# The first gate/up pair by seven products, the frames' sums made earlier, the last forms spread

## The chip, the cores and the metric

The kernel runs on one core of one Trainium2 chip, in one launch. The metric is device time in microseconds (us), the median of several executions. All times below are us unless marked otherwise.

## The reference

One layer of a hybrid streaming encoder, for 512 prompt frames and 64 frames of a running stream (576 in all), D = 2048 channels, everything in float32:

```python
hn   = rmsnorm(x, g_norm1);  proj = hn @ w_in          # 2048 x 6144: q, k, v and three convolution inputs
o    = concat(rmsnorm(attention(q, k, v)), rmsnorm(gated short convolution))
x    = x + o @ w_out                                    # 2048 x 2048
h2   = rmsnorm(x, g_norm2)
x    = x + (silu(h2 @ w_gate) * (h2 @ w_up)) @ w_down   # D_FF = 5632
```

The change touches what lies between `x + o @ w_out` and the start of `@ w_down`.

## The kernel before, in words

**Precision.** A float32 matmul is made as three matmuls in the fast fp32r form: each operand is split into a high part and a rest, and high x high, rest x high, high x rest are summed in PSUM. `split` makes both parts: ACT casts the high part (L231), DVE subtracts it from the source (L232). Every weight block and every frame block passes through it.

**Seven products.** The 576 frames are taken in two halves of 288, and a unit of work is 256 columns of weights. Weights, frames and results are cut in 2 x 2 blocks, and the four blocks of the result are made from seven products (Strassen's scheme in Winograd's form) instead of eight. A product has 8 k-tiles of three matmuls, 24 matmuls of 128x128 by 128x288 (L406). It uses a sum of weight blocks and a sum of frame blocks. The weight sums are made for every unit on DVE (`weight_sums`, L344 to L354, four sums of 128x1024). The frame sums are made once for all gate and up units: t1 and t2 (tile `t12`, products 5 and 6) and t3 and t4 (`t34`, products 7 and 4).

**Order.** TensorE's order is written by hand: a list `order` of pairs (unit, product). `prepare(n, p)` issues loads, sums and splits of the weights of a product, and runs four entries ahead (`AHEAD`) of `run(n, p)`, which issues the matmuls and what follows them: a product's bank is copied out by ACT (`part`, L429), added by DVE to the other product of its result block, and given to `finish`. `Pipeline` spreads other work between the matmuls: it counts a tick for every three matmuls, and a generator that is spawned there goes on after as many ticks as it yields. The order on ACT, DVE, GpSimd and SP's DMA queue is set by a scheduler from its own costs, apart from the end (from product 1 of unit NGU-1, the last up unit, on), where all of them keep program order (`manual_schedule`). Every engine works its list in order.

**Feed-forward stage.** Gate and up units alternate, so pair `fp` has a gate and an up unit. `finish` scales a result block by the row scale R2 of the second RMSNorm, applies Silu for gate, and multiplies up by gate. `put_forms` then builds the seven sums ("forms") of the hidden block that the down projection will need, splits each into a 128x2x288 tile and stores it to DRAM (`hid_dram`, 288 KB each); they come back in loads of 2016 KB as the down units need them (SBUF doesn't hold them all). For the last pair, the forms with index over 3 are split into tiles that later are accumulators of the down stage (`spare`: `acc_ax`, `acc_t`, `acc_z`).

**Around the change.** `out_proj` (for the second half of channels, `mixa`) runs over eight blocks of 256 output channels, two channel tiles each, for both halves of frames, 96 matmuls a block; a result leaves through one of three PSUM banks by two DVE steps (L1022, L1023: scale and residual). `after_b2(kt)` then makes the high and low parts of the scaled x (h2: also the block b12), its square, and a running sum of squares on GpSimd (L1259), and stores x to DRAM for the later residual. Behind `out_proj` pair 0 of gate/up is made by eight full products in `wide` (L1391, 384 matmuls, four weight blocks of their own), with R2 made by `row_scale2` in between and the generator `frame_sums` making t12 and t34, one pair of channel tiles every nine ticks. Only then comes the loop over `order`, whose first two units are written interleaved:

```python
order = [(0, 1), (0, 2), (1, 1), (1, 2), (0, 6), (0, 7), (0, 5), (0, 3), (0, 4), (1, 6), (1, 7), (1, 5)]
```

Units of `w_in`, earlier in the kernel (numbers below zero, stage A), run through the same helpers; their first two units are interleaved too (`early=True`: product 3 has a bank `psv` of its own).

Of the kernel before, what the change touches and what calls it, by code (L numbers as in the profile page):

```python
# [10 lines left out]
F32 = mybir.dt.float32  # L11
# [90 lines left out]
def tile_hybrid_stream_step(  # L102
# [47 lines left out]
    for w in (w_gate, w_up):  # L150
        for kk in range(2):
            specs.append((w[kk * 1024 : (kk + 1) * 1024, 0:256].rearrange("(k p) c -> p k c", p=P), 8, 256))
# [190 lines left out]
    def weight_sums(n):  # L343

        st, m, tt = unit[n], UNITS[n][3], nc.vector.tensor_tensor
        st["a21"], st["a22"] = (region[n, 1][0][:, :, q, :] for q in range(2))
        st["s1"] = spool[0].tile([P, NP, P], F32, tag="s1", name="s1")[:, :m]
        tt(out=st["s1"], in0=st["a21"], in1=st["a22"], op=ALU.add)
        yield
        tt(out=st["a21"], in0=st["a21"], in1=st["a11"], op=ALU.subtract)  # L350
        yield
        tt(out=st["a11"], in0=st["s1"], in1=st["a11"], op=ALU.subtract)
        yield 6
        tt(out=st["a12"], in0=st["a12"], in1=st["a11"], op=ALU.subtract)  # L354
        yield 3
# [67 lines left out]
    def run(n, p_, early=False):  # L423
# [589 lines left out]
    def out_proj(frame, R, after=None):  # L1013
        for c in range(D // 256):
            whi, wlo = next_weight()
            load_x2()
            for j in range(2):
# [219 lines left out]
    b12pool = tc.alloc_tile_pool(name="b12pool", bufs=1, reuse_waits="tile", side="left")  # L1237
    b12h = b12pool.tile([P, NP, HALF], F32R, name="b12h")
    b12l = b12pool.tile([P, NP, HALF], F32R, name="b12l")
    acc2 = [b12pool.tile([P, HALF], F32, name=f"acc2_{i}") for i in range(2)]  # L1240

    def h2(kt, i):
        if i == 0:
            return h2a[kt]
        return b22s[kt // 2] if kt % 2 else (b12h[:, kt // 2, :], b12l[:, kt // 2, :])

    def after_b2(kt):
        for i, (a, b) in enumerate(HALVES):
            hi, lo = h2(kt, i)
            src = x2(kt)[:, a:b]  # L1250
            nc.scalar.activation(out=hi, in_=src, func=AF.Copy, scale=col("g2", kt))
            nc.vector.scalar_tensor_tensor(out=lo, in0=src, scalar=col("g2", kt), in1=hi.bitcast(F32),
                                           op0=ALU.mult, op1=ALU.subtract)
# [13 lines left out]
    parts2 = []  # L1267
    for i in range(2):
        sh, sl = parts("sq2")
        split(sh, sl, acc2[i])  # L1270
        parts2.append((sh, sl))
# [12 lines left out]
    t12z = tpool.tile([P, 2, 2, HALF], F32R, tag="t12z", name="t12z")  # L1284
    t34 = []
# [5 lines left out]
    turn = [0]  # L1291

    def ps_tile(name):
        turn[0] += 1
        if turn[0] % 2:
            return ps_pj.tile([P, HALF], F32, tag="pj", name=name)
        return ps_z.tile([P, 512], F32, tag=f"z{turn[0] // 2 % 3}", name=name)[:, :HALF]

    def frame_sums():

        for j in range(NP):
            ev, od = x2(2 * j), x2(2 * j + 1)
            ge, go = col("g2", 2 * j), col("g2", 2 * j + 1)
            b11 = tmp.tile([P, HALF], F32, tag="ms", name="b11", bufs=1)
            b22 = tmp.tile([P, HALF], F32, tag="t", name="b22", bufs=1)
            nc.scalar.activation(out=b11, in_=ev[:, :HALF], func=AF.Copy, scale=ge)
            nc.scalar.activation(out=b22, in_=od[:, HALF:], func=AF.Copy, scale=go)
            ta = b12pool.tile([P, 2, HALF], F32, tag="ta", name="ta")
            tb = b12pool.tile([P, 2, HALF], F32, tag="tb", name="tb")
            t1, t2, t3, t4 = ta[:, 0], ta[:, 1], tb[:, 0], tb[:, 1]  # L1310
            nc.vector.scalar_tensor_tensor(out=t1, in0=ev[:, HALF:], scalar=ge, in1=b11, op0=ALU.mult, op1=ALU.subtract)
            nc.gpsimd.tensor_tensor(out=t2, in0=b22, in1=t1, op=ALU.subtract)
            nc.vector.scalar_tensor_tensor(out=t3, in0=ev[:, HALF:], scalar=ge, in1=b22, op0=ALU.mult, op1=ALU.subtract)
            nc.vector.scalar_tensor_tensor(out=t4, in0=od[:, :HALF], scalar=go, in1=t2, op0=ALU.mult, op1=ALU.subtract)
            two = t12[:, :, j] if j < NP - 1 else t12z
            split(two[:, :, 0, :], two[:, :, 1, :], ta)
            t34.append(ypool.tile([P, 2, 2, HALF], F32R, tag=f"y{j}", name=f"t34_{j}"))
            split(t34[j][:, :, 0, :], t34[j][:, :, 1, :], tb)
            yield 9

# [3 lines left out]
    spare = []  # L1324

    def put_form(fp, n, src):

        if fp == NFP - 1 and n > 3:
            t = spare.pop(0)()
        else:  # L1330
            t = tmp.tile([P, 2, HALF], F32R, tag="hl", name="form")
# [28 lines left out]

    def finish(kind, fp, c, i, ps, part=None):
# [8 lines left out]
        else:  # L1370
            nc.vector.tensor_tensor(out=s, in0=ps, in1=part, op=ALU.add)  # L1371
            nc.vector.tensor_tensor(out=s, in0=s, in1=R2[:, a:b], op=ALU.mult)
        if kind == "gate":
            nc.scalar.activation(out=s, in_=s, func=AF.Silu)
            return
# [4 lines left out]
    def wide(kind, hold=None):  # L1380

        pss = {}
        for kk in range(2):
            whi, wlo = next_weight()
            for i, j in ((1, 0), (1, 1), (0, 0), (0, 1)):
                if kk == 0:
                    pss[j, i] = ps_tile("pw")
                for k in range(8):
                    xh, xl = h2(8 * kk + k, i)
                    for n, (w_, x_) in enumerate(((whi, xh), (wlo, xh), (whi, xl))):  # L1390
                        mm(pss[j, i], w_[:, k, j * P : (j + 1) * P], x_,  # L1391
                           start=(kk == 0 and k == 0 and n == 0), stop=(kk == 1 and k == 7 and n == 2))
                    pipe.tick()
                if kk == 1:
                    finish(kind, 0, j, i, pss[j, i])
            if hold and kk == 0:
                hold()
# [45 lines left out]
    down = {}  # L1443

    def take_blocks(d):

        if d in (0, 3):
# [17 lines left out]
    def spare_tile(name, q):  # L1465

        if name not in down:
            pool, n, tag = {"z": (h2pool, 6, "z"), "t": (tpool, 4, "t12z"), "ax": (down["pool"], 2, "ax")}[name]
            down[name] = pool.tile([P, n, HALF], F32, tag=tag, name=f"acc_{name}")
        return down[name][:, 2 * q : 2 * q + 2, :].bitcast(F32R)  # L1470

    for name, q in (("ax", 0), ("t", 0), ("t", 1), ("z", 2)):
        spare.append(lambda name=name, q=q: spare_tile(name, q))
# [64 lines left out]
    for k_ in range(AHEAD):  # L1538
        prepare(*order[k_])
    for k_, (n, p_) in enumerate(order):  # L1540
# [5 lines left out]
        run(n, p_)  # L1546
# [62 lines left out]
```

## Time and profile before

| | |
|---|---|
| median of 3 runs | 2394.09 (2393.43 to 2395.15) |
| profiled execution, its own time | 2397.15 |
| span of its trace | 2395.4 |
| granted TensorE clock, mean | 0.995 |
| instructions in the span | 43789 |
| TensorE matmuls | 17609, busy 2350.2 |

Stages by the trace: units of w_in from about 80 to 600, attention and the first half of `out_proj` to 784, the second half to 886.70, `wide` to 938.18, seven-product units of gate/up to about 1880, down units to about 2388.

How to read the rows. In a row of time order stand start, duration, engine, line, operation, output<-input, tile size, count, and in brackets the idle time ahead of it and what ended it. In a group (line first) stand the count, busy time and mean ns of one, then the idle time ahead and what ended it. In a row of windows stand the stretch, its length, busy time and count of TensorE, of its weight loads, of DVE, ACT and GpSimd, the granted clock, the busy share of the DMA engines and GB/s. In a wait stand who waits, for whom, total, times, longest. In a DMA row stand issues, KB each, and median us from issue to landing. Matmul durations overlap (each row shows about 0.29 while one starts every 0.132), so the length of a group is its count times 0.132. A 288-wide step is 128 partitions by 288 elements.

### The profile page before, as it was taken

What the parts mean: (1) busy time and instruction counts of PE and PEld (TensorE: products, weight loads), DVE (VectorE), ACT (ScalarE), POOL (GpSimd) and SP (SyncE); (2) the same over time, 40 slices, a digit from 0 to 9 for tenths busy, and PEclk for the clock granted to TensorE, in tenths of its full rate; (3) what the DMA queues carried; (4) which work ended last, traced back from release to release, by engine and by line L of the source; (5) the groups of instructions that cost most, each with busy time, mean ns of one, the idle gap of its engine ahead of it and who ended that gap; (6) DMA issues with size and microseconds to landing.
All of it is one profiled execution on the core that took longest, in us unless ns stands there. A gap on an engine that the chain in (4) does not pass through costs nothing.

```text
span 2395.4 us, 43789 instructions
## 1 busy us (share of the span) xinstructions
PE 2350.2 (98%) x17609; PEld 2336.2 (98%) x17609; DVE 1934.0 (81%) x2828; ACT 1234.6 (52%) x2211; POOL 300.3 (13%) x377
## 2 busy tenths in 40 slices
PE   8899999999999999999999999999999899999998
PEld 8899999999899999999999999999999899999998
DVE  7888888787677768888888888888888768887875
ACT  7456656455777545444444444444444444444454
POOL 0111121120233221000000000000000002431211
PEclk9999999999999999999999999999999999999999
DMA  7433343525733333444444444345354936875642
GB/s 254 141 113 104 114 138 89 162 88 188 236 105 104 107 135 106 141 150 132 139 151 142 129 150 153 118 156 159 109 157 139 338 111 212 225 222 194 204 129 79
DMA packets 474900, 360.60 MB, mean 151 GB/s; under 512 B 11278, under 2 KB 460680, under 8 KB 474696
## 3 DMA queue, kind: packets, MB, share of 16 engines
q1 hardware_dynamic: 469528, 351.02, 45.8%
q0 software_dynamic: 5168, 6.79, 1.6%
q8 instruction: 138, 2.26, 0.4%
q14 instruction: 66, 0.54, 0.1%
HBM read 281.39 MB, written 76.37 MB: 149 GB/s over the span
## 4 chain that ended last, share of the span: by engine, by line
PE 82%; DVE 6%; ACT 4%; issue 2%; DMA 1%; POOL 1%; SPq 0%; DVEq 0%; ACTq 0%; POOLq 0%
PE psy L406 43%; PE psw L406 21%; PE psx L406 10%; PE pjo L227 5%; DVE whl L232 1%; DMA v_dram<-tok 1%; PE pw L1391 1%; ACT whl L231 1%; ACT ph L231 0%; PE pot L1514 0%; DVE c L881 0%; ACT whi L179 0%; DMA raw_a<-in_w_down_dram 0%; DVE raw_b L350 0%; DVE wlo L180 0%
## 5 line engine op out<-in xcount | busy, mean ns | idle before, releaser
L232 DVE TENSOR_TENSOR whl<-raw_a,whl 128x1024 fp32r<-128x1024 f32 (+4 forms) x376 | 424.6, 1130 | 70.2 <-ACT whl L231 68.5
L406 PE MATMUL psy<-t,whl 128*128 128x288 f32 x2916 | 437.3, 295 | 0.5 <-ACT part L429 0.5
L231 ACT CAST whl<-raw_a 128x1024 fp32r<-128x1024 f32 (+4 forms) x376 | 352.3, 938 | 141.4 <-PE psx L406 52.1
L406 PE MATMUL psy<-h_s,whl 128*128 128x288 f32 x2724 | 411.8, 295 | 6.8 <-ACT part L429 6.8
L406 PEld LDWEIGHTS psy<-t,whl 128*128 128x128 f32 x2916 | 403.4, 189 | 0.9 <-ACT part L429 0.7
L406 PEld LDWEIGHTS psy<-h_s,whl 128*128 128x128 f32 x2724 | 378.7, 189 | 7.3 <-ACT part L429 7.3
L406 PE MATMUL psw<-t,whl 128*128 128x288 f32 x2592 | 377.2, 295 | 0.0
L406 PEld LDWEIGHTS psw<-t,whl 128*128 128x128 f32 x2592 | 354.0, 189 | 0.2
L232 DVE TENSOR_TENSOR whl<-raw_b,whl 128x1024 fp32r<-128x1024 f32 (+5 forms) x230 | 247.7, 1077 | 89.3 <-ACT whl L231 87.8
L231 ACT CAST whl<-raw_b 128x1024 fp32r<-128x1024 f32 (+5 forms) x230 | 207.2, 903 | 208.2 <-PE psw L406 70.0
L429 ACT COPY part<-psy 128x288 f32<-128x288 f32 x303 | 120.8, 399 | 350.0 <-PE psy L406 345.4
L406 PE MATMUL psx<-h_s,whl 128*128 128x288 f32 x1122 | 166.8, 297 | 2.7 <-DVE gs L1371 2.7
L406 PEld LDWEIGHTS psx<-h_s,whl 128*128 128x128 f32 x1122 | 156.2, 191 | 2.9 <-issue 2.9
L231 ACT CAST whl<-s 128x1024 fp32r<-128x1024 f32 (+5 forms) x101 | 93.3, 924 | 119.9 <-PE psw L406 114.1
L406 PE MATMUL psy<-t12a,whl 128*128 128x288 f32 x1056 | 150.0, 295 | 2.0 <-ACT part L429 2.0
L406 PE MATMUL psw<-t34a,whl 128*128 128x288 f32 x1056 | 150.4, 295 | 1.4 <-DVE ghs L869 0.9
L406 PEld LDWEIGHTS psy<-t12a,whl 128*128 128x128 f32 x1056 | 143.2, 188 | 2.7 <-ACT part L429 2.7
L406 PEld LDWEIGHTS psw<-t34a,whl 128*128 128x128 f32 x1056 | 143.4, 188 | 1.9 <-DVE ghs L869 1.1
L232 DVE TENSOR_TENSOR whl<-s,whl 128x1024 fp32r<-128x1024 f32 (+5 forms) x101 | 107.5, 1065 | 19.9 <-ACT whl L231 18.1
L227 PE MATMUL pjo<-mixc,whi 128*128 128x288 f32 x512 | 119.4, 300 | 0.0
L1334 POOL DMA_DIRECT2D hid_dram<-form x3 | 2.4, 807 | 923.9 <-DVE form L232 923.9
L227 PE MATMUL pjo<-mixa,whi 128*128 128x288 f32 x512 | 102.7, 295 | 0.0
(599 smaller groups left out, 4138.4 us busy)
## 6 DMA issues: line engine op xcount, KB each, us to landing
hid_dram<-form SPq DMA_DIRECT2D x147, 288.0 KB, 2.3
raw_a<-in_w_gate_dram SPq DMA_DIRECT2D x23, 1024.0 KB, 6.4
raw_a<-in_w_up_dram SPq DMA_DIRECT2D x23, 1024.0 KB, 6.0
raw_a<-in_w_in_dram SPq DMA_DIRECT2D x22, 1024.0 KB, 5.5
raw_b<-in_w_in_dram SPq DMA_DIRECT2D x22, 1024.0 KB, 8.2
raw_b<-in_w_gate_dram SPq DMA_DIRECT2D x21, 1024.0 KB, 6.7
raw_b<-in_w_up_dram SPq DMA_DIRECT2D x21, 1024.0 KB, 7.8
h_s<-hid_dram SPq DMA_DIRECT2D x10, 2016.0 KB, 9.9
```

The lines of the kernel that those rows point to most:

```text
L227: mm(ps, w_[:, k, csl], x_[:, a:b], start=(k == 0 and n == 0), stop=(k == nk - 1 and n == 2))
L231: cast = nc.scalar.copy(out=hi, in_=src)
L232: (lo_eng or nc.vector).tensor_tensor(out=lo, in0=src, in1=hi.bitcast(F32), op=ALU.subtract)
L406: mm(ps, whl[:, w_, j, :], x_, start=(start and j == 0 and q == 0), stop=(j == len(xs_) - 1 and q == 2), skip_group_check=True)
L429: nc.scalar.copy(out=t, in_=st["y"])
L1334: q.dma_start(out=hid_dram[fp][2 * n - 2 : 2 * n].rearrange("f p t -> p f t"), in_=t.bitcast(F32))
L1391: mm(pss[j, i], w_[:, k, j * P : (j + 1) * P], x_, start=(kk == 0 and k == 0 and n == 0), stop=(kk == 1 and k == 7 and n == 2))
```

## The change

1. Pair 0 goes through seven products like all others: it becomes units 0 and 1, `wide` and its four weight blocks go, and the other units move up by two in number. Units 0 and 1 are interleaved by a new list. Their weights are loaded by `before_b2` inside `out_proj` (the B halves in block 3, the A halves in the last two blocks), and two products are prepared and two weight sums made there.
2. `frame_sums` is called per pair of channel tiles inside `out_proj` (five ticks after the second tile of a pair, then in steps of four ticks). The split t12 forms of seven pairs go to a DRAM buffer (14 stores of 288 KB) and come back in two loads of 2016 KB (`load_t12`, ticks 3 and 9 of the new stage); t34 is written in place of the x tile of its pair, which waits for the store of x. Pair 7 is made directly in SBUF, its t2 on DVE instead of GpSimd. The b12 block is no longer split. x is stored per pair.
3. `row_scale2` starts at tick 19 of the new stage, with one plain fp32 matmul of ones for each half, and a shorter chain (Identity, Ln, Exp, Square on ACT, two steps on DVE).
4. Unit 0's product 2 is finished six ticks later; unit 1's product 2 goes to a spare bank z2, and its product 3 to the bank `misc`.
5. The last pair's forms 2, 5, 7, 6 and 4 are made by a generator, `last_forms`, from 34 ticks after the last finish on, then every 10 ticks, inside the down stage; they use the ordinary form tiles, and `spare` goes.

The diff, cut to its core:

```diff
-    for w in (w_gate, w_up):
-        for kk in range(2):
...
-    gu = [(kind, fp, 0, NP) for fp in range(1, NFP) for kind in ("gate", "up")]
+    gu = [(kind, fp, 0, NP) for fp in range(NFP) for kind in ("gate", "up")]
...
-            x = ps_z.tile([P, 512], F32, tag="z0", name="psx2")[:, :HALF]
+            x = ps_z.tile([P, 512], F32, tag="z2" if n == 1 else "z0", name="psx2")[:, :HALF]
             multiply(x, n, 2, True)
+            if n == 0:
+                def later_done():
+                    yield 6
+                    done(0, 0, x, st["p1"])
+
+                pipe.spawn(later_done())
+                return
             add(0, 0, x, st["p1"])
...
-            st["u2"] = kept("ms" if n == NGU - 1 else "t")
+            st["u2"] = kept("ms" if n in (0, NGU - 1) else "t")
...
-            st["v"] = ps_pj.tile([P, HALF], F32, tag="pj", name="psv")
+            st["v"] = misc("psv")[:, :HALF] if n == 1 else ps_pj.tile([P, HALF], F32, tag="pj", name="psv")
...
+    def frame_sums(j):
+        ev, od = x2(2 * j), x2(2 * j + 1)
+        ge, go = col("g2", 2 * j), col("g2", 2 * j + 1)
+        b11 = tmp.tile([P, HALF], F32, tag="ms", name="b11", bufs=1)
+        b22 = tmp.tile([P, HALF], F32, tag="t", name="b22", bufs=1)
+        nc.scalar.activation(out=b11, in_=ev[:, :HALF], func=AF.Copy, scale=ge)
+        nc.scalar.activation(out=b22, in_=od[:, HALF:], func=AF.Copy, scale=go)
+        t1, t2 = (tmp.tile([P, HALF], F32, tag="y", name="ta") for _ in range(2))
+        t3, t4 = (tmp.tile([P, HALF], F32, tag="r", name="tb") for _ in range(2))
+        nc.vector.scalar_tensor_tensor(out=t1, in0=ev[:, HALF:], scalar=ge, in1=b11, op0=ALU.mult, op1=ALU.subtract)
+        z = j == NP - 1
+        (nc.vector if z else nc.gpsimd).tensor_tensor(out=t2, in0=b22, in1=t1, op=ALU.subtract)
+        nc.vector.scalar_tensor_tensor(out=t3, in0=ev[:, HALF:], scalar=ge, in1=b22, op0=ALU.mult, op1=ALU.subtract)
+        yield 4
+        nc.vector.scalar_tensor_tensor(out=t4, in0=od[:, :HALF], scalar=go, in1=t2, op0=ALU.mult, op1=ALU.subtract)
+        for q, t in enumerate((t1, t2)):
+            form = down["t12z"][:, q] if z else tmp.tile([P, 2, HALF], F32R, tag="hl", name="t12f")
+            split(form[:, 0], form[:, 1], t)
+            if not z:
+                nc.sync.dma_start(out=t12_dram[q, j], in_=form.bitcast(F32))
+        yield 4
+        t34.append(ypool.tile([P, 2, 2, HALF], F32R, tag=f"y{j}", name=f"t34_{j}"))
+        for q, t in enumerate((t3, t4)):
+            split(t34[j][:, q, 0], t34[j][:, q, 1], t)
...
-        if kt % 4 == 3:
-            m = kt // 4
-            for k in (4 * m, 4 * m + 2):
-                nc.sync.dma_start(out=x2_dram[k : k + 2].rearrange("k p t -> p k t"), in_=x2t[k // 2])
-
-    out_proj(lambda k: mixa[k], accA, after_b2)
+        if kt % 2:
+            nc.sync.dma_start(out=x2_dram[kt - 1 : kt + 1].rearrange("k p t -> p k t"), in_=x2t[kt // 2])
+            pipe.spawn(frame_sums(kt // 2), 5)
+        if kt == KD - 2:
+            prepare(0, 1)
+            prepare(0, 2)
+            for _ in range(2):
+                one_sum(0)
+    def before_b2(c):
+        if c == 3:
+            load_columns([("B", 0), ("B", 1)])
+        elif c == D // 256 - 2:
+            load_columns([("A", 0)])
+        elif c == D // 256 - 1:
+            load_columns([("A", 1)])
+    out_proj(lambda k: mixa[k], accA, after_b2, before_b2)
...
     def row_scale2():
+        yield 19
         for i, (a, b) in enumerate(HALVES):
-            ss = channel_sums(*parts2[i], a, b, "ss2")
-            rsqrt_mean(R2[:, a:b], ss, D, HALF)
-
+            ss = misc("ss2")[:, :HALF]
+            mm(ss, oner.bitcast(F32), acc2[i], start=True, stop=True)
+            y, t = (tmp.tile([P, HALF], F32, tag=tag, name="y2") for tag in ("y", "r"))
+            nc.scalar.activation(out=ss, in_=ss, func=AF.Identity, scale=1.0 / D, bias=epsc)
+            nc.scalar.activation(out=y, in_=ss, func=AF.Ln)
+            nc.scalar.activation(out=y, in_=y, func=AF.Exp, scale=-0.5)
+            nc.scalar.activation(out=t, in_=y, func=AF.Square)
+            nc.vector.scalar_tensor_tensor(out=t, in0=t, scalar=-0.5, in1=ss, op0=ALU.mult, op1=ALU.mult)
+            nc.vector.scalar_tensor_tensor(out=R2[:, a:b], in0=t, scalar=1.5, in1=y, op0=ALU.add, op1=ALU.mult)
+        apool.release()
+    pipe.spawn(row_scale2())
...
+    def load_t12():
+        yield 3
+        for q in (1, 0):
+            nc.sync.dma_start(out=t12[:, q].bitcast(F32), in_=t12_dram[q].rearrange("j p f t -> p j f t"))
+            yield 6
+    pipe.spawn(load_t12())
...
+    def last_forms(s10):
+        fp, h, tt = NFP - 1, hid.pop(NFP - 1), nc.vector.tensor_tensor
+        s00, s01, s11 = h[0, 0], h[0, 1], h[1, 1]
+        yield 34
+        tt(out=s01, in0=s01, in1=gates.pop((0, 1)), op=ALU.mult)
+        yield 5
+        tt(out=s10, in0=s10, in1=R2[:, :HALF], op=ALU.mult)
+        tt(out=s10, in0=s10, in1=gates.pop((1, 0)), op=ALU.mult)
+        for n, out, a, b in ((2, s10, None, None), (5, s00, s01, s00), (7, s01, s01, s11), (6, s11, s11, s00),
+                             (4, s10, s10, s11)):
+            yield 10
+            if a is not None:
+                tt(out=out, in0=a, in1=b, op=ALU.subtract)
+            put_form(fp, n, out)
...
+            if kind == "up" and fp == NFP - 1 and (c, i) == (1, 0):
+                pipe.spawn(last_forms(s))
+                return
             nc.vector.tensor_tensor(out=s, in0=s, in1=R2[:, a:b], op=ALU.mult)
+        if kind == "up" and fp == NFP - 1 and (c, i) == (0, 1):
+            hid[fp][c, i] = s
+            return
...
-    pipe.spawn(frame_sums(), 20)
-    wanted += [(0, 0), (1, 0), (0, 1), (1, 1)] + [(n, c) for n in range(2, NGU) for c in range(2)]
-    wanted += [(n, None) for n in range(NGU, NU)]
-    wide("gate", row_scale2)
-    load_columns([("A", 0)])
-    wide("up", lambda: load_columns([("A", 1)]))
-    pipe.flush()
-    b12pool.release()
-    w2pool = tc.alloc_tile_pool(name="w2pool", bufs=1, reuse_waits="tile", side="left")
-    spool[0] = w2pool
-    raw_tile["B"] = w2pool.tile([P, 2, 2048], F32, name="raw_b")
-    load_columns([("B", 0), ("B", 1)])
...
-    order = [(0, 1), (0, 2), (1, 1), (1, 2), (0, 6), (0, 7), (0, 5), (0, 3), (0, 4), (1, 6), (1, 7), (1, 5)]
-    for n in range(1, NU):
+    order = [(0, 1), (0, 2), (1, 1), (1, 2), (0, 3), (0, 6), (1, 3), (0, 5), (0, 7), (1, 6),
+             (0, 4), (1, 5), (1, 7), (2, 1), (1, 4), (2, 2), (2, 6), (2, 7), (2, 5)]
+    early = {0, 1}
+    for n in range(2, NU):
...
-    for k_ in range(AHEAD):
+    for k_ in range(2, AHEAD):
-        run(n, p_)
+        run(n, p_, n in early)
```

More of the change, by code (lines that the diff above doesn't have):

```diff
@@ L347, in weight_sums @@
         st["s1"] = spool[0].tile([P, NP, P], F32, tag="s1", name="s1")[:, :m]
-        tt(out=st["s1"], in0=st["a21"], in1=st["a22"], op=ALU.add)
+        s = tt(out=st["s1"], in0=st["a21"], in1=st["a22"], op=ALU.add)
+        if n == 2:
+            tc.keep_in_program_order(s)
         yield
@@ L1011, in x2, with out_proj @@
         return x2t[kt // 2][:, kt % 2, :]
-    def out_proj(frame, R, after=None):
+    def out_proj(frame, R, after=None, before=None):
         for c in range(D // 256):
@@ L1016, in out_proj @@
             load_x2()
+            if before:
+                before(c)
             for j in range(2):
@@ L1236, in tile_hybrid_stream_step @@
     b22s = [(places[2 * k], places[2 * k + 1]) for k in range(KD, KD + NP)]
[L1237 to L1245, printed above, removed]
+    w2pool = tc.alloc_tile_pool(name="w2pool", bufs=1, reuse_waits="tile", side="left")
@@ new lines, in tile_hybrid_stream_step @@
+    spool[0] = w2pool
+    raw_tile["B"] = w2pool.tile([P, 2, 2048], F32, name="raw_b")
+    w2pool.tile([P, NP, P], F32, tag="s1", name="s1_0")
+    apool = tc.alloc_tile_pool(name="apool", bufs=1, reuse_waits="tile", side="left")
+    acc2 = [apool.tile([P, HALF], F32, name=f"acc2_{i}") for i in range(2)]
+    wanted += [(0, 1), (1, 1), (0, 0), (1, 0)] + [(n, c) for n in range(2, NGU) for c in range(2)]
+    wanted += [(n, None) for n in range(NGU, NU)]
+    down = {}
+    t12_dram = tc.dram_tile([2, NP - 1, P, 2, HALF], F32, name="t12_dram")
@@ L1289, in frame_sum @@
         return t34[j][:, q, f, :] if p_ in (7, 4) else t12[:, q, j, f, :] if j < NP - 1 else t12z[:, q, f, :]
[L1291 to L1319, printed above, removed]
     gates = {}
     hid = {}
-    spare = []
     def put_form(fp, n, src):
[L1328 to L1331, printed above, removed]
+        t = tmp.tile([P, 2, HALF], F32R, tag="hl", name="form")
         split(t[:, 0], t[:, 1], src)
@@ L1442, in tile_hybrid_stream_step @@
     acc = {}
-    down = {}
     def take_blocks(d):
+        if "z" not in down:
+            open_blocks()
         if d in (0, 3):
@@ L1463, in take_blocks, with open_blocks @@
             acc[d, q // 2, q % 2] = ap
[L1465 to L1468 removed]
+    def open_blocks():
+        for name, pool, n, tag in (("z", h2pool, 6, "z"), ("t", tpool, 4, "t12z"), ("ax", down["pool"], 2, "ax")):
             down[name] = pool.tile([P, n, HALF], F32, tag=tag, name=f"acc_{name}")
[L1470 to L1473 removed]
     def add_residual(d):
```

36 lines of the change are left out of this document (7 added, 29 removed).

## The prediction

> **What bounds the kernel now.** I read the page first (busy time by engine, the chain that ended last), then TensorE's waits, then TensorE's instructions in order of time around the three places that the change touches: the start of the feed-forward stage, the output projection ahead of it, and the turn from gate/up to down.
>
> ```profile
> PE 2350.2 (98%) x17609; PEld 2336.2 (98%) x17609; DVE 1934.0 (81%) x2828; ACT 1234.6 (52%) x2211; POOL 300.3 (13%) x377
> PE 82%; DVE 6%; ACT 4%; issue 2%; DMA 1%; POOL 1%; SPq 0%; DVEq 0%; ACTq 0%; POOLq 0%
> ...
> PE psy L406 <- ACT part L429: 9.8, 7, 6.3
> PE psx L406 <- DVE gs L1371: 2.7, 1, 2.7
> ```
>
> TensorE is busy 98% of the span: only fewer matmuls, or its few stalls, can bring time. Of the waits (total, times, longest), a single 6.3 and a single 2.7 stand beside the change. Each stands at a seam, and each is followed by a slow stretch. The first seam, in TensorE's order of time, in the window of 5 us behind it, and as the chain of waits sees it:
>
> ```profile
> 886.70 0.29 PE L1391 MATMUL pw<-b12h,whi 128*128 128x288 f32 x1
> ...
> 938.18 2.94 PE L406 MATMUL psy<-h_s,whl 128*128 128x288 f32 x21
> ...
> 951.00:956.00 5.00, 5.00 (x23) 5.00 (x22) 4.03 (x5) 1.60 (x3) 0.00 (x0) 0.50 0.34 119
> ...
> 950.52 6.10 PE psx L406 x24
> 956.62 3.25 PE psy L406 x24
> ...
> 966.71 3.48 PE psy L406 x24
> ...
> 973.36 3.17 PE psy L406 x24
> ```
>
> The wide products of pair 0 fill 886.70 to 938.18. A product of 24 matmuls takes 3.17 where nothing waits (last row), 0.132 a matmul. From 938.18 to 973.36 lie nine products, 28.53 by that row, in 35.18: **6.65 lost**. Of that, the wait for `gs` makes 2.7, and the half clock behind it (granted clock 0.50, 23 matmuls in 5 us) makes 6.10 - 3.17 = 2.9. The second seam:
>
> ```profile
> 1879.58 0.55 PE L406 MATMUL psx<-t,whl 128*128 128x288 f32 x3
> 1886.45 1.81 PE L406 MATMUL psy<-h_s,whl 128*128 128x288 f32 x6 [6.32 <-ACT part L429]
> ...
> 1892.15 0.56 PE L406 MATMUL psy<-t,whl 128*128 128x288 f32 x3
> 1892.55 0.98 PE L406 MATMUL psy<-h_s,whl 128*128 128x288 f32 x6
> ...
> 1876.10 0.43 ACT L231 CAST acc_ax<-ut 128x288 fp32r<-128x288 f32 x1 [2.26 <-DVE ut L1342]
> ...
> 1880.85 0.51 ACT L231 CAST whl<-raw_a 128x384 fp32r<-128x384 f32 x1 [1.66 <-DVE raw_a L352]
> ...
> 1885.25 0.43 ACT L231 CAST acc_z<-ux 128x288 fp32r<-128x288 f32 x1 [1.01 <-DVE ux L1342]
> ...
> 1886.00 0.39 ACT L429 COPY part<-psy 128x288 f32<-128x288 f32 x1
> 1879.60 0.55 DVE L350 TENSOR_TENSOR raw_a<-raw_a 128x384 f32<-128x384 f32 x1
> ```
>
> The last two products before it need only `part` out of bank `psy`. ACT gets to it at 1886.00, because the forms of the last pair (`acc_ax`, `acc_t`, `acc_z`) stand ahead in its fixed order, each waiting for a DVE step; DVE gets to the sum of L350 only at 1879.60 for the same reason. The 27 matmuls from 1886.45 to 1892.55 took 6.10 instead of 3.57. Loss: 6.32 + 2.53 = **8.85**.
>
> **The change part by part.**
>
> *Fewer matmuls.* 384 wide ones become 14 products of 24, 336. The four matmuls of L287 become two in plain fp32, which go in two passes each, so I count them as equal. 48 x 0.132 = **-6.35**. These lie on the path.
>
> *The first seam goes.* Pair 1 no longer follows a stage of another shape: **-6.65**. What is late next is the interleaved start itself, now units 0 and 1, right behind the output projection. Where another interleaved start is in the trace (units of w_in, 87 to 135 us) it went like this:
>
> ```profile
> 102.01 3.48 PE L406 MATMUL psy<-t12a,whl 128*128 128x288 f32 x24 [0.55 <-ACT part L429]
> 105.97 3.44 PE L406 MATMUL psv<-bod,whl 128*128 128x288 f32 x24 [0.49 <-ACT part L429]
> ...
> 113.44 3.44 PE L406 MATMUL psw<-t34a,whl 128*128 128x288 f32 x24 [0.86 <-DVE ghs L869]
> ...
> 120.54 3.44 PE L406 MATMUL psy<-t12a,whl 128*128 128x288 f32 x24 [0.49 <-ACT part L429]
> ```
>
> Four waits, 2.39, and four products longer by 0.27 to 0.31: 3.5 in all. That is the low bound. But ACT and DVE have other work in their queues there, so I walk the printed order of the changed kernel's instructions with these durations:
>
> ```profile
> 948.05 0.45 DVE L232 TENSOR_TENSOR form<-ut,form 128x288 fp32r<-128x288 f32 x1
> 948.42 1.22 DVE L232 TENSOR_TENSOR whl<-raw_a,whl 128x1024 fp32r<-128x1024 f32 x1
> 949.55 0.45 DVE L232 TENSOR_TENSOR form<-ux,form 128x288 fp32r<-128x288 f32 x1
> ...
> 941.56 1.05 ACT L231 CAST whl<-raw_a 128x1024 fp32r<-128x1024 f32 x1
> L278 ACT ACTIVATE y<-ms 128x288 f32<-128x288 f32 x2 | 0.9, 442 | 2.2 <-DVE ms L277 2.2
> ```
>
> From start to start DVE needs 0.37 for a 288-wide step (0.45, its whole duration, where it needs the step before) and 1.13 for a 1024-wide one. Six products from 886.70, with 0.53 for the square sums, end at 886.70 + 19.02 + 0.53 = 906.3. The seventh is unit 1's product 3. Its weight halves stand on DVE behind the whole of R2: the square sums come at tick 19 of three matmuls, 886.7 + 7.5, and end near 895; ten ACT steps of 0.34 to 0.44 and two DVE steps follow, so R2 is ready near 900.1. Behind it in DVE's order come four sums and three weight splits, 7 x 1.13, and five 288-wide steps, 5 x 0.45: the seventh product's low half is ready at 900.1 + 7.9 + 2.3 = 910.3, with the waits for ACT's casts 911. **+4.6** for that wait, and **+2.7** for a half clock behind it (between the 2.9 and the 2.53 above).
>
> A second one: unit 2's product 6 needs DVE, after unit 1's product 4 ends, to do a finish, two sums, a split, a gate step, another finish and the split of its own weights, 4 x 1.13 + 4 x 0.45 = 6.3, while only one product of 3.17 runs meanwhile: **+3.2**. Whether the clock drops there as well I count at half, **+1.35**: the walk is good to about 1.5, the 0.86 in stage A cost no clock, and 2.7 did.
>
> The Trainium skill's page "TensorE: Matmul & The Clock Gate", Part 1, says that the clock falls to half after one idle window of about 3.4 us. The trace disagrees on the length: 2.7 idle sufficed here. By the page's rule the second wait would cost no clock and the sum would be 1.35 lower.
>
> *What moves into the output projection.* Per pair three multiply-subtracts and four splits on DVE, less one b12 split, and seven of eight POOL steps; its stores and R2's inputs go out with it:
>
> ```profile
> 785.00:835.00 50.00, 50.00 (x376) 49.79 (x375) 36.98 (x71) 26.08 (x58) 11.04 (x14) 1.00 0.36 120
> 835.00:886.00 51.00, 51.00 (x387) 51.00 (x386) 34.36 (x64) 22.24 (x48) 13.05 (x17) 1.00 0.37 130
> ...
> L1311 DVE SCALAR_TENSOR_TENSOR ta<-x,vec,b 128x288 f32<-128x288 f32 x7 | 3.6, 511 | 0.0
> L1312 POOL TENSOR_TENSOR ta<-b,ta 128x288 f32<-128x288 f32 x8 | 8.6, 1081 | 32.3 <-DVE ta L1311 26.4 <-ACT gs L1374 3.0 <-ACT whl L231 2.8
> 942.19 1.06 DVE L232 TENSOR_TENSOR form<-ut,form 128x288 fp32r<-128x288 f32 x1
> ```
>
> A column block c is 96 matmuls, 12.69. DVE is busy (36.98 + 34.36) / 101 of it, 8.96. New: 2 x 0.51 + 4 x 0.45 = 2.8, so 11.8 (0.5 less by start to start). It fits, and TensorE, which has three banks between it and the eviction, waits for nothing: **0**. If this cover is gone, each microsecond over 12.69 counts eight times, since every later DVE step, R2 among them, stands behind it.
>
> A rule speaks against this: the page "SBUF — State Buffer" of the Trainium skill (on the two sides of its ports) says that GpSimd and a DVE step with two SBUF inputs take one port pair in turn, the loser waiting out the whole instruction. The row of 942.19 agrees, a 0.45 step taking 1.06 beside a POOL one. With 1.08 of POOL more in each block DVE would need at most 12.9 and end 1.7 late; the sum would be 1.7 higher.
>
> The stores of the t12 sums and the two loads back are 288 KB and 2016 KB pieces:
>
> ```profile
> hid_dram<-form SPq DMA_DIRECT2D x147, 288.0 KB, 2.3
> ...
> h_s<-hid_dram SPq DMA_DIRECT2D x10, 2016.0 KB, 9.9
> ...
> h_s<-hid_dram SPq DMA_DIRECT2D x1, 2016.0 KB, 18.6
> ```
>
> The first load, at tick 3, lands near 898 by the 9.9 row and is needed by the sixth product at 903.1; the second near 905, needed after 909. On SP the last x2 store stands just behind the first load, and ACT's split of t34_7 waits for that store, in front of R2's Exp. Cost between 0 and some 4 us; I take 0, for the store is 576 KB and the DMA share in the two rows above is 0.37.
>
> *The second seam.* In the printed order the sums of L350 and the copy of `part` now stand ahead of all forms; `part` comes as soon as its product ends. **-8.85**, less what the queue takes back: DMA is full there (the 18.6 us row is the load of that window, against 9.9 elsewhere), TensorE now arrives 8.85 earlier, and by my count the weights of the third down unit land only about 2 us before their use. Take-back between 0 and 4, taken at **+1.35** with the forms' steps between the down units' splits.
>
> Sum: -6.35 - 6.65 + 4.6 + 2.7 + 3.2 + 1.35 - 8.85 + 1.35 = **-8.65**. The profiled execution took 2397.15 (span 2395.4), 3.06 over the median of the three runs, 2394.09; the sum from it is 2388.5, from the median **2385.4**.
>
> **The rivals.**
>
> *It starts like stage A.* If the scheduler's order lets DVE slip the seventh product's weights in earlier than my walk has it, the start costs 3.5 instead of 11.85: -17.0, **2377**. For it: the same order of products and the same helper. Against it: R2 stands in the queue.
>
> *The waits only move.* The last forms' steps or the down weights come late by the same 8.85 that TensorE gains, since their DMA bytes are the same: the second seam gives 0 to 1, the rest as forecast: **2393**. For it: the 18.6 row. Against it: in the trace nothing of this seam waits for a DMA.
>
> *Slower: DVE full in the output projection.* If a block needs p over 12.69, DVE ends it 8 x (p - 12.69) late, whether TensorE's banks show it there or R2 and the seventh product pay later. It decides from p = 12.69 + 8.65 / 8 = 13.8; at 14.5 it is +14.5, **2400**. For it: the 1.06 row; if all 32 POOL sums of squares and the moved steps each hit a two-input step, that is near. Against it: 11.8 by the rows.
>
> *It does not do what it says.* The count of matmuls falls by 48 in any order, so at most the waits change: this is in the cases above.
>
> **How the numbers follow.** Forecast 0.52, with its own range 2381 to 2391 (second half clock or none, take-back 0 to 4, walk 1.5); like stage A 0.20; waits only move 0.15; slower 0.13. The range 2374 to 2396 leaves out the slower case and tails. About 0.2%, 4.8 us, is what a measurement of this kernel can tell: under 2389.3 is faster, over 2398.9 slower. Faster: 0.20 + 0.50 = 0.70; same 0.15 + 0.02 = 0.17; slower 0.13.
>
> **What would show it.** Right: about 48 matmuls fewer; a wait of 4 to 5 near 906 ahead of unit 1's product 3, ended by the weight split or its cast, with a granted clock near 0.5 behind it; one of 2 to 4 some ten products later; no wait over 1 between the last gate/up product and the second down unit; no stall before 886. Wrong: TensorE idle inside the output projection, DVE over 95% there, R2 later than 902, a DMA as releaser near 1885 to 1900.

## Result: 3.6 us less, and the profile after

| | before | after |
|---|---|---|
| median of 21 runs each | 2395.15 (2392.54 to 2400.18) | 2391.51 (2388.01 to 2395.40) |
| ratio, 95% interval | 1 | 0.9982 [0.9977, 0.9988] |
| profiled execution, its own time | 2397.15 | 2391.99 |
| span of its trace | 2395.4 | 2390.3 |

The changed kernel is 3.64 us faster, 0.15% (the ratio of the runs says 0.18%), where 8.65 were forecast. The interval leaves out 1, so the gain is real. The time lies inside the range given, but the gain is under the 0.2% that was called faster: the change did less than half of what was predicted.

The page of the changed kernel, its engines, and TensorE's waits from 880 to 1920 us (total, times, longest). Line numbers are each kernel's own: the matmuls of L406, the casts and subtractions of L231 and L232 and the copy of L429 are here L404, L227, L228 and L427.

```profile
PE 2346.2 (98%) x17561; PEld 2331.7 (98%) x17561; DVE 1949.8 (82%) x2845; ACT 1241.0 (52%) x2225; POOL 300.3 (13%) x376
...
PE psv L404 <- ACT whl L227: 4.6, 1, 4.6
PE psy L404 <- ACT whl L227: 2.8, 1, 2.8
PE psy L404 <- DVE whl L228: 0.9, 1, 0.9
PE psv L404 <- DVE whl L228: 0.8, 1, 0.8
PE psy L404 <- ACT part L427: 0.5, 1, 0.5
```

The trace counts exactly 48 matmuls fewer. The waits of 6.3 and 2.7 of before are gone; 4.6 + 0.85 and 2.8 + 0.93 have come, both for weight splits (`whl`). In TensorE's order of time (start, duration, instruction, count, idle time ahead):

```profile
887.36 2.97 PE L404 MATMUL psy<-h_s,whl 128*128 128x288 f32 x21
...
893.75 1.82 PE L404 MATMUL psy<-h_s,whl 128*128 128x288 f32 x12
895.41 1.13 PE L1320 MATMUL ss<-acc,oner 128*128 128x288 f32 x4
896.16 1.56 PE L404 MATMUL psy<-h_s,whl 128*128 128x288 f32 x9
...
897.97 2.93 PE L404 MATMUL psx<-h_s,whl 128*128 128x288 f32 x21
...
907.08 0.56 PE L404 MATMUL psy<-t12z,whl 128*128 128x288 f32 x3
912.24 0.41 PE L404 MATMUL psv<-h_z,whl 128*128 128x288 f32 x1 [4.60 <-ACT whl L227]
913.50 0.85 PE L404 MATMUL psv<-h_z,whl 128*128 128x288 f32 x2 [0.85 <-DVE whl L228]
914.14 5.24 PE L404 MATMUL psv<-h_s,whl 128*128 128x288 f32 x21
919.18 3.01 PE L404 MATMUL psy<-t,whl 128*128 128x288 f32 x21
...
947.42 0.55 PE L404 MATMUL psx<-h_z,whl 128*128 128x288 f32 x3
950.78 0.61 PE L404 MATMUL psy<-t,whl 128*128 128x288 f32 x1 [2.81 <-ACT whl L227]
952.32 4.95 PE L404 MATMUL psy<-t,whl 128*128 128x288 f32 x20 [0.93 <-DVE whl L228]
...
957.50 3.37 PE L404 MATMUL psw<-t,whl 128*128 128x288 f32 x24
...
1880.98 0.95 PE L404 MATMUL psy<-h_s,whl 128*128 128x288 f32 x6
...
2382.10 0.82 PE L1519 MATMUL pot<-ident,acc 128*128 128x128 f32 x6
```

Both waits stand where the walk put them: ahead of the seventh product (unit 1's product 3), and ten products later ahead of unit 2's product 6. Around each the windows show why:

```profile
887.00:912.00 25.00, 20.64 (x152) 20.18 (x151) 23.96 (x36) 16.29 (x30) 3.41 (x3) 1.00 0.70 244
914.00:919.00 5.00, 5.00 (x23) 5.00 (x23) 0.58 (x1) 0.00 (x0) 0.00 (x0) 0.50 0.71 210
930.00:945.00 15.00, 15.00 (x115) 15.00 (x115) 9.30 (x15) 5.19 (x10) 2.42 (x3) 1.00 0.39 125
952.00:957.00 5.00, 4.68 (x20) 4.69 (x21) 3.84 (x7) 0.88 (x3) 1.65 (x1) 0.51 0.31 112
```

The fourth number of each row is DVE's busy time. Ahead of the first wait DVE is full, 23.96 of 25; ahead of the second it is not, 9.30 of 15. So the two have different causes. Behind each the granted clock is 0.50 or 0.51 for 5 us.

The weights of unit 1's product 3 are the last of its four sums (L352). The cast of 911.14 on ACT, whose end ends the first wait, waits for that sum, and the cast ahead of it waits for the sum before:

```profile
909.88 1.04 ACT L227 CAST whl<-raw_a 128x1024 fp32r<-128x1024 f32 x1 [1.75 <-DVE raw_a L350]
911.14 1.05 ACT L227 CAST whl<-raw_a 128x1024 fp32r<-128x1024 f32 x1 [0.21 <-DVE raw_a L352]
```

So ACT is not what is late there. The weights of unit 2's product 6 need the first three of its sums. The first of them stands on DVE behind the forms of pair 0, whose casts on ACT wait for stores of form tiles:

```profile
944.19 0.43 ACT L227 CAST form<-ut 128x288 fp32r<-128x288 f32 x1 [1.16 <-DMA hid_dram<-form]
...
945.03 1.22 DVE L344 TENSOR_TENSOR s<-raw_b 128x1024 f32<-128x1024 f32 x1
```

The output projection, with the frame sums in it, lost nothing:

```profile
785.00:835.00 50.00, 50.00 (x377) 49.79 (x376) 43.54 (x85) 29.73 (x68) 13.34 (x15) 1.00 0.57 181
835.00:886.00 51.00, 51.00 (x386) 51.00 (x386) 44.48 (x85) 29.04 (x64) 17.38 (x19) 1.00 0.51 172
```

TensorE is busy throughout, DVE 87% (88.02 of 101, or 11.06 of a block's 12.69). At the turn to the down units the row of 1880.98 above is the first of a stretch without any wait over 0.5. From there to the transposes of the last output (the row of 2382.10) it is 501.12. The same stretch of the kernel before is 509.89:

```profile
1877.60 0.95 PE L406 MATMUL psy<-h_s,whl 128*128 128x288 f32 x6
...
2387.49 0.82 PE L1514 MATMUL pot<-ident,acc 128*128 128x128 f32 x6
```

### The profile page after: what moved, and what is told of

Same layout as the page of the kernel before. It is cut to its first block, busy times and chain, and to the rows that moved or that the text cites. A ratio compares the mean times of both kernels' runs of the same rounds, so it can differ in the third digit from the quotient of the medians.

```text
span 2390.3 us, 43795 instructions
## 1 busy us (share of the span) xinstructions
PE 2346.2 (98%) x17561; PEld 2331.7 (98%) x17561; DVE 1949.8 (82%) x2845; ACT 1241.0 (52%) x2225; POOL 300.3 (13%) x376
## 5 line engine op out<-in xcount | busy, mean ns | idle before, releaser
L228 DVE TENSOR_TENSOR whl<-raw_a,whl 128x1024 fp32r<-128x1024 f32 (+4 forms) x384 | 434.9, 1134 | 67.5 <-ACT whl L227 65.6
L404 PE MATMUL psy<-t,whl 128*128 128x288 f32 x3000 | 451.3, 296 | 4.2 <-ACT whl L227 2.8
L227 ACT CAST whl<-raw_a 128x1024 fp32r<-128x1024 f32 (+4 forms) x384 | 360.6, 941 | 137.1 <-PE psx L404 48.0
L404 PEld LDWEIGHTS psy<-t,whl 128*128 128x128 f32 x3000 | 416.6, 189 | 5.2 <-ACT whl L227 3.0
L404 PE MATMUL psy<-h_s,whl 128*128 128x288 f32 x2766 | 417.0, 295 | 0.5 <-ACT part L427 0.5
L404 PE MATMUL psw<-t,whl 128*128 128x288 f32 x2688 | 390.2, 295 | 0.0
L404 PEld LDWEIGHTS psy<-h_s,whl 128*128 128x128 f32 x2766 | 383.2, 188 | 1.0 <-ACT part L427 0.9
L404 PEld LDWEIGHTS psw<-t,whl 128*128 128x128 f32 x2688 | 366.7, 188 | 0.2
L228 DVE TENSOR_TENSOR whl<-raw_b,whl 128x1024 fp32r<-128x1024 f32 (+5 forms) x234 | 256.1, 1095 | 95.4 <-ACT whl L227 94.4
L227 ACT CAST whl<-raw_b 128x1024 fp32r<-128x1024 f32 (+5 forms) x234 | 211.4, 905 | 222.3 <-PE psw L404 74.0
L427 ACT COPY part<-psy 128x288 f32<-128x288 f32 x309 | 123.2, 399 | 356.2 <-PE psy L404 351.2
L404 PE MATMUL psx<-h_s,whl 128*128 128x288 f32 x1164 | 170.3, 294 | 0.0
L404 PEld LDWEIGHTS psx<-h_s,whl 128*128 128x128 f32 x1164 | 159.6, 188 | 0.0
L227 ACT CAST whl<-s 128x1024 fp32r<-128x1024 f32 (+5 forms) x103 | 95.4, 926 | 117.7 <-PE psw L404 114.0
L404 PE MATMUL psy<-t12a,whl 128*128 128x288 f32 x1056 | 150.0, 295 | 2.0 <-ACT part L427 2.0
L404 PE MATMUL psw<-t34a,whl 128*128 128x288 f32 x1056 | 150.5, 295 | 1.4 <-DVE ghs L874 0.9
L404 PEld LDWEIGHTS psy<-t12a,whl 128*128 128x128 f32 x1056 | 143.1, 188 | 2.6 <-ACT part L427 2.6
L404 PEld LDWEIGHTS psw<-t34a,whl 128*128 128x128 f32 x1056 | 143.5, 188 | 1.9 <-DVE ghs L874 1.1
L228 DVE TENSOR_TENSOR whl<-s,whl 128x1024 fp32r<-128x1024 f32 (+5 forms) x103 | 109.8, 1066 | 18.6 <-ACT whl L227 17.1
```

Source lines behind the costliest of these rows:

```text
L227: cast = nc.scalar.copy(out=hi, in_=src)
L228: (lo_eng or nc.vector).tensor_tensor(out=lo, in0=src, in1=hi.bitcast(F32), op=ALU.subtract)
L404: mm(ps, whl[:, w_, j, :], x_, start=(start and j == 0 and q == 0), stop=(j == len(xs_) - 1 and q == 2), skip_group_check=True)
L427: nc.scalar.copy(out=t, in_=st["y"])
```

## The experiments

Each kernel differs from one of the two by the lines shown. Ratios are against the kernel before on the same chip; medians of before in the two sets were 2395.73 and 2394.52, so differences are taken from these.

**Part 5 alone, on the kernel before.** The edit is the change's `last_forms`, its two branches in `finish`, and `open_blocks` in place of `spare`; nothing else:

```diff
+            if kind == "up" and fp == NFP - 1 and (c, i) == (1, 0):
+                pipe.spawn(last_forms(s))
+                return
...
-        if fp == NFP - 1 and n > 3:
-            t = spare.pop(0)()
```

> The kernel before with part 5 of the change alone (the last pair's forms spread into the down stage). Theory, by the two traces: the whole gain of the change at the second seam (8.77 in the profiled executions) comes from this part and stands by itself. Expected: no wait for part near 1880, no half clock behind it, 8 to 9 less than before, about 2386.5. Rival: part of that gain came from the other parts (units renumbered, loads shifted): under 6 less. That would be faster than the changed kernel as a whole (2391.5).

Measured: 2387.03, ratio 0.9962 [0.9950, 0.9975], 8.70 less than before. TensorE's waits from 880 to 1920:

```profile
PE psx L406 <- DVE gs L1381: 2.7, 1, 2.7
PE psy L406 <- ACT part L429: 0.9, 2, 0.5
```

The 6.3 is gone, the 2.7 of the first seam is left as it was. The gain at the second seam stands by itself, and this part alone is faster than the whole change by some 5 us.

**The change without part 5.** The same lines the other way.

> The changed kernel without part 5 (forms of the last pair made as before, in tiles that later are accumulators). Theory: the first units' part of the change gains nothing, it costs 2 to 5; so this kernel has the wait near 1883 and its half clock back and comes to 2391.5 + 8.8 = 2400, slower than before by 3 to 5. Rival: the first units' part gains by itself and the seam gives less than the trace says: under 2395.

Measured: 2399.88, ratio 1.0012 [1.0004, 1.0021], 4.15 slower than before. The waits in the same window:

```profile
PE psy L404 <- ACT part L427: 6.3, 1, 6.3
PE psv L404 <- ACT whl L227: 3.5, 1, 3.5
PE psy L404 <- ACT whl L227: 2.8, 1, 2.8
```

So parts 1 to 4 together, with 48 matmuls fewer, cost about 4 us; part 5 brings about 8.

**Another order of products.**

```diff
-    order = [..., (0, 3), (0, 6), (1, 3), (0, 5), (0, 7), (1, 6),
+    order = [..., (0, 3), (0, 6), (0, 5), (0, 7), (1, 3), (1, 6),
```

> The changed kernel with one edit: in the list of products, unit 1's product 3 stands behind unit 0's products 5 and 7 instead of ahead of them. Theory: TensorE waits 5.45 (4.60 + 0.85) there because DVE works without a gap from 886 to 914 on steps that stand ahead of this product's weights; products 5 and 7 of unit 0 have their weights ready earlier and fill 6.3 of that. Expected: the wait shrinks from 5.45 to 0.7 for the copy of part between products 6 and 5, plus 0 to 0.5, no half clock behind it: 7 to 8 less than the changed kernel, about 2384. Rival: the wait is set by R2's chain, and every product behind it waits for DVE in turn: the same wait one or two products later, under 2 less.

Measured: 2384.51, ratio 0.9951 [0.9939, 0.9964]: 11.22 under before, 7.58 more than the changed kernel brought. In order of time:

```profile
907.61 3.08 PE L404 MATMUL psy<-t,whl 128*128 128x288 f32 x21 [1.11 <-ACT part L427]
...
914.11 0.56 PE L404 MATMUL psv<-h_z,whl 128*128 128x288 f32 x3
```

Product 3 of unit 1 now follows at 914.11 without a wait, and the 1.11 for `part` is all that is left of the first wait. The rival (the wait moves on to the next product) falls: DVE had enough done by then. The second wait is still there (2.76 + 0.93).

**The sums of unit 1 left out.** Unsummed blocks stand in place of the sums. The scheduler then also places the split of unit 1's product 3 ahead of that of unit 0's product 5, so the test takes away both DVE's time and the place in the queue:

```diff
+            if n == 1:
+                st["s1"], st["summed"] = st["a21"] if "a21" in st else region[n, 1][0][:, :, 0, :], 3
+                st["a21"], st["a22"] = (region[n, 1][0][:, :, q, :] for q in range(2))
             while st["summed"] != 3:
                 one_sum(n)
```

> The changed kernel without the four weight sums of unit 1 (its products use unsummed weights; this part of the computation is left out). 4 x 1.13 less on DVE ahead of product 3's weights. Theory (DVE's work ahead of these weights sets the first wait): the wait of 5.45 falls to under 1 and its half clock goes, 8 less, about 2383.5. Rival (ACT's copy of part and the table load ahead of the cast set it): the cast still comes late, the wait stays at 2 to 3 with its half clock: 3 less.

Measured: 2383.17, ratio 0.9952 [0.9938, 0.9966]: 11.35 under before, 7.7 more than the changed kernel. The first wait is gone. This run alone doesn't settle the rival, since the cast now stands ahead of ACT's copy and table load as well. The changed kernel's trace does: both casts there wait for the sums of L350 and L352 (the rows of 909.88 and 911.14 above). With these rows, this run and the run before, the first wait is shown to come from the DVE work ahead of these weights.

**The sums of unit 2 earlier.**

```diff
             prepare(*order[k_ + AHEAD])
+        if k_ == 9:
+            for _ in range(3):
+                one_sum(2)
```

> The changed kernel with one edit: three of the weight sums of unit 2 are placed earlier in the program, right after unit 2's first weights are split (four products ahead of where they were). Theory: the second wait (2.81 + 0.93 ahead of unit 2's product 6, at 950.8) comes from these sums standing on DVE behind the forms of pair 0, which wait for GpSimd and for stores of form tiles, while DVE idles from 930 to 945; their loads had landed by 928. Expected: that wait and the half clock behind it go, 6.5 less in all, about 2385. Rival: the loads land late or DVE is full there: the wait stays, or comes back at another product, under 2 less.

Measured: 2386.51, ratio 0.9956 [0.9942, 0.9969]: 9.22 under before, 5.6 more than the changed kernel. On DVE the sums now run at

```profile
931.77 1.22 DVE L344 TENSOR_TENSOR s<-raw_b 128x1024 f32<-128x1024 f32 x1
...
933.28 1.22 DVE L348 TENSOR_TENSOR raw_b<-raw_b,raw_a 128x1024 f32<-128x1024 f32 x1
...
934.78 1.22 DVE L350 TENSOR_TENSOR raw_a<-s,raw_a 128x1024 f32<-128x1024 f32 x1
```

instead of from 945.03 on, and the wait and its half clock are gone; a wait of 0.45 for `part` is new. The loads were not late: the sums could run 13 us earlier. The second wait was one of place in the queue alone. The change itself asks for that place, in two lines of `weight_sums` that none of its five parts names:

```diff
+        if n == 2:
+            tc.keep_in_program_order(s)
```

`s` is the first sum of unit 2 (L344), which by these lines keeps its place in the program's order. No run leaves these lines out, so whether the scheduler would have placed this sum earlier by itself is not shown.

**The differences of pair 0's forms on DVE.**

```diff
-            (nc.vector if fp else nc.gpsimd).tensor_tensor(out=out, in0=a, in1=b, op=op)
+            nc.vector.tensor_tensor(out=out, in0=a, in1=b, op=op)
```

> The changed kernel with pair 0's differences of forms on DVE, as for all other pairs, instead of GpSimd. Theory: the second wait comes from where unit 2's sums stand, behind the forms, and of that chain the trips to GpSimd are the smaller part beside the waits for the stores of form tiles: the wait of 3.74 shrinks by 1 at most and the half clock stays: 0 to 1.5 less. Rival: GpSimd's 0.8 to 1.65 us steps and their sharing with DVE hold the chain up: the wait falls under 1.5 and its half clock goes, 5 less.

Measured: 2389.41, ratio 0.9982 [0.9973, 0.9992]: 5.11 under before, 1.5 more than the changed kernel by the medians; the ratio to the kernel before is the changed kernel's own, 0.9982, so no gain is shown. The second wait is 2.32 + 1.14 instead of 2.81 + 0.93:

```profile
948.32 0.40 PE L404 MATMUL psy<-t,whl 128*128 128x288 f32 x1 [2.32 <-ACT whl L227]
949.85 4.43 PE L404 MATMUL psy<-t,whl 128*128 128x288 f32 x20 [1.14 <-DVE whl L228]
```

The half clock stays. GpSimd is the smaller part of that chain; the forms ahead still wait for their casts on ACT, and two of those for stores of form tiles (0.33 and 0.88).

**Both edits together, the order and the sums of unit 2.**

> Both edits together: unit 1's product 3 behind unit 0's products 5 and 7, and unit 2's three sums earlier. If the two waits are independent, their gains add: 7.0 and 5.0 under the changed kernel's 2391.5, so 2379.5. Rival: with the first wait gone TensorE reaches unit 2's product 6 some 8 earlier, and its weights (loads, sums) are late again: about 2384.

Measured: 2378.78, ratio 0.9930 [0.9918, 0.9942], 15.74 under before. The gains nearly add (7.58 + 5.58 over the changed kernel's 3.64 make 16.8). This kernel beats both, and does about what the prediction's rival "It starts like stage A" said of the change (-17.0): TensorE's waits at the start are now

```profile
905.96 3.08 PE L404 MATMUL psy<-t,whl 128*128 128x288 f32 x21 [0.66 <-ACT part L427]
...
944.79 3.04 PE L404 MATMUL psy<-t,whl 128*128 128x288 f32 x21 [0.44 <-ACT part L427]
```

**The same with unit 0's product 7 ahead of its product 5.**

> As the kernel with both edits, but unit 0's product 7 ahead of its product 5, so that the copy of part between products 6 and 5 (the wait of 1.11 left in the first of them) lies under a product of another bank. Theory: 0.7 to 1.1 less, about 2378.5. Rival: product 7's weights, made only behind R2, are then the late ones: no gain or a new wait.

Measured: 2379.54, ratio 0.9936 [0.9923, 0.9948], 14.98 under before. The wait at product 5 is gone in the trace, the one near 945 is 0.64 instead of 0.44, and the time is the same within the intervals: the expected 0.7 to 1.1 did not show.

## Why the prediction was wrong

The forecast was -8.65. The places of the waits and the steps that end them were right; the prices of the start were not. Parts 1 to 4 were forecast at -1.15 and cost 4.15 where they were measured without part 5. Part 5 was forecast at -7.5 and brought 8.70 alone. From the seams of the two profiled executions, term by term (a product is 3.17):

| term | forecast | profiled executions |
|---|---|---|
| 48 matmuls | -6.35 | -6.35 (17561 against 17609) |
| first seam's loss gone | -6.65 | -6.65 (the wait for `gs` is gone) |
| sums of squares in plain fp32 | 0 | +0.52 |
| first wait | +4.6 | +5.45 (4.60 + 0.85) |
| half clock behind it | +2.7 | +3.08 |
| second wait | +3.2 | +3.74 (2.81 + 0.93) |
| half clock behind it | +1.35 | +2.77 |
| second seam | -7.5 | -8.77 |
| sum | -8.65 | -6.21 |

The measured terms: unit 1's product 1, the third product, takes 897.97 - 893.75 = 4.22 with the sums of squares in it, so these cost 1.05, not the 0.53 of the four matmuls that they replace. From 907.48, where the sixth product ends, to 919.18 are 11.70 for one product, 8.53 lost, 5.45 of it waiting. From 947.82 to 957.50 are 9.68, 6.51 lost, 3.74 of it waiting.

*The step that failed most* within the table is "Whether the clock drops there as well I count at half". The walk had this wait at 3.2, and a wait of 2.66 in the kernel before had been followed by a granted clock of 0.50. The wait of 2.81 and 0.93 brought 0.51 and the full 2.77, +1.42 of the miss. With the other order of products the 1.11 at 907.61 is followed by 21 matmuls in 3.08, no half clock.

*The first seam's price was that of one execution.* The prediction took its 6.65 whole from one trace (6.49 by the starts in time order, 938.18 to 973.20), with 2.9 of it for a half clock. The same wait of 2.67 in the kernel with part 5 alone brought none: the granted clock stayed at 1.00, and nine products lost 3.75. Here is the row in the kernel before, then in that kernel; behind them the same pair for a wait that stands far ahead of the change:

```profile
950.52 5.38 PE L406 MATMUL psx<-h_s,whl 128*128 128x288 f32 x21 [2.66 <-DVE gs L1371]
951.86 3.04 PE L406 MATMUL psx<-h_s,whl 128*128 128x288 f32 x21 [2.67 <-DVE gs L1381]
...
561.09 0.75 PE L805 MATMUL ssg<-accc,oner 128*128 128x288 f32 x2 [2.19 <-DVE yt L792]
561.28 1.33 PE L805 MATMUL ssg<-accc,oner 128*128 128x288 f32 x2 [2.18 <-DVE yt L792]
```

So a wait of 2.2 to 2.7 costs a half clock in one execution and none in another. With 3.75 for the first seam the terms add up to -3.31; the measured -3.64 lies between that and -6.21. How often the half clock comes at this seam is not measured.

The Trainium skill's "TensorE: Matmul & The Clock Gate", Part 1, puts the idle window at about 3.4 us. The half clocks behind waits of 2.18 and 2.66 are under that, and the measurement decides: in this kernel a wait from 2.76 us up was followed by a half clock each time, one of 2.2 to 2.7 some of the time.

*The two waits*, +0.85 and +0.54. For the first, the walk had R2 ready at 900.1; DVE started the last steps of its two halves only at 901.66 and 902.76, so R2 was whole at 903.2. That is later than 902, which the prediction had named as a sign of being wrong. What stood behind R2 on DVE was as walked: four sums, three splits and five steps of 288.

```profile
886.88 1.43 POOL L1295 TENSOR_TENSOR acc<-acc,sq 128x288 f32<-128x288 f32 x1 [0.32 <-ACT sq L1294]
887.58 1.06 DVE L1266 SCALAR_TENSOR_TENSOR ta<-x,vec,b 128x288 f32<-128x288 f32 x1
...
901.17 0.45 DVE L1326 SCALAR_TENSOR_TENSOR y<-y,ss 128x288 f32<-128x288 f32 x1
901.66 0.46 DVE L1327 SCALAR_TENSOR_TENSOR R<-y,y 128x288 f32<-128x288 f32 x1
...
902.76 0.45 DVE L1327 SCALAR_TENSOR_TENSOR R<-y,y 128x288 f32<-128x288 f32 x1
```

DVE ran without a longer gap than 0.61 from 886 to this point, on the last evictions, two weight sums, four weight splits and the last pair's sums. The prediction added up R2's own steps and did not see that they would stand behind this work, nor that ACT's Ln would wait for DVE, for a tile that a t12z split still read:

```profile
898.70 0.41 ACT L1323 ACTIVATE y<-ss 128x288 f32<-128x288 f32 x1 [0.67 <-DVE t12z L228]
```

For the second wait, DVE had three sums to do behind unit 1's product 4, not two: from that product's end at 944.64 to the end of the split at 952.27 are 7.63, where the walk had 6.3. Nor did the walk see that DVE idles for 5.70 of the 15 us before, in which these sums could have been made.

*The sums of squares*, +0.52: "which go in two passes each, so I count them as equal" is wrong. The trace shows two records for each of the two plain fp32 matmuls, but together they take twice what four of the others do.

*The second seam* was better than forecast by 1.27: the take-back of 1.35 that was allowed for the full DMA queue did not come; nothing waits for a load there.

The sum by terms is -6.21; between the two executions the span differs by 5.1, because the changed kernel started its output projection 0.6 later (a wait for cached keys of 3.2 against 2.5, far ahead of the change) and ended its tail 0.3 longer, and because 6.65 is 6.49 by the starts. The medians differ by 3.64: before's profiled execution lay 2.0 above its median of 21, after's 0.5. The executions of one kernel differ in their mean granted clock. Of 30 further executions of the kernel before, ten at 0.996 took 2392.73 to 2394.57 and 17 at 0.995 took 2394.01 to 2398.34. That fits half clocks that come in some executions only; at which waits they came there is not shown.

*The rivals.* "It starts like stage A", at 0.20, was not what this kernel does, but about what it does once the order and the sums of unit 2 are changed. "The waits only move" is refuted: part 5 alone keeps its 8.7. "DVE full in the output projection" had the right engine and the wrong place: there DVE took 11.06 of 12.69 a block, and TensorE lost nothing; it is full from 887 to 912 instead. The Trainium skill's "SBUF — State Buffer" (its two sides) says that a DVE step with two SBUF inputs and a GpSimd step that reads SBUF take a shared port pair in turn. The DVE step of 1.06 at 887.58 (0.51 on average in the kernel before) beside a GpSimd one of 1.43 agrees, but it decided nothing: TensorE lost nothing in the output projection, and at the second wait moving pair 0's forms off GpSimd brought at most 1.5.

## What to carry to other kernels

When a stage ends and another starts, the vector engine works through a burst (evictions of the old stage, operands of the new one). A list of products that ran well in a steady state can starve there, so order the first products by when their operands come out of that burst, not by what frees a bank. A step that stands late in its engine's queue runs late, even when its inputs are ready and the engine idles: look for idle time of the engine ahead of the wait to tell the two cases apart. Price every stall on TensorE of about 2.8 us or more with its half-clock tail of 2 to 3 us. For one of 2.2 to 2.7 us the tail is a matter of odds, and a loss read from one execution may hold a tail that the median has not.

## What the runs showed of the hardware

In the ten traces, from 60 us on, each wait of TensorE from 2.76 to 6.32 us was followed by a half clock (0.50 granted for some 3 to 7 us; 2.0 to 3.1 us lost on top of the wait where the change is). None of up to 1.82 us that stands by itself was. Between them it differed: the wait of 2.18 to 2.19 us near 561 was followed by it in four traces and not in six, waits of 2.56, 2.60, 2.64 and 2.66 were, and waits of 2.54 and 2.67 were not. Two plain fp32 matmuls of 128x128 by 128x288 took 1.05 us, four fp32r ones of the same tile 0.53. A 1024-wide cast on ACT (1.05) and its subtraction on DVE (1.22) in turn make the pair of waits, first ACT's and then DVE's 0.65 to 1.14, that marks a weight split coming late.
